# Eight start places for the split-weight buffers of a two-layer decoder kernel

## The chip, the cores and the metric

One core of a Trainium2 chip runs the whole program. The metric is device time in microseconds. Before the change the median of three runs is 1462.51 us (1461.71 to 1464.09).

## The reference

Two layers of a decoder trunk work on 512 tokens of width 1024, all in float32. What matters here is that nearly all the arithmetic is matrix products with weights:

```python
def hybrid_layer(x, g_mix, w_in, sinks, w_a, w_b, w_out, g_mlp, w_up, w_down):
    h = rmsnorm(x, g_mix)
    z = h @ w_in                       # 1024 x 5888, split into nine parts
    ...
    ya = sliding_window_sink_attention(aq, ak, av, sinks) @ w_a
    ...
    r = chunkwise_retention(rq, rk, rv)
    r = r * lax.rsqrt(jnp.mean(r * r, axis=-1, keepdims=True) + EPS)
    r = r.reshape(B, S, RET_V) * jax.nn.silu(rg.astype(jnp.float32))
    yb = r.astype(x.dtype) @ w_b
    mixed = jax.nn.sigmoid(ga) * ya + jax.nn.sigmoid(gb) * yb
    x = x + mixed @ w_out
    h2 = rmsnorm(x, g_mlp)
    x = x + jnp.square(jax.nn.relu(h2 @ w_up)) @ w_down
    return x
```

A last normalisation follows the second layer.

## The kernel before, in words

**Products.** Each float32 operand is split into a high part, rounded to the format `F32R`, and a low part, the rest. A product of two split operands is three matmuls, high by high, high by low and low by high (`products`, lines 390, 391 and 392; line 1296 for one of the matrices, line 405 in `by_halves`). Every matmul has two operands in SBUF: 128 x 128 **weights**, which TensorE loads first (the profile's PEld), and a **moving** operand of up to 512 columns, which it then streams through (the profile's PE). In the profile's names the moving operand stands first: `mm<-xh,hi` streams the activations `xh` past weights from `hi`, and `mm<-hi,r` streams weights of the model, `hi`, past activations in `r`. Weights of the next matmul are loaded while the present one streams.

**Units.** The model's weights come in units of 128 x 1024 numbers. The function `unit_order` writes their order out by hand. `split_until` (line 320) keeps three units ahead of the one in use: SyncE loads a unit into a `raw` buffer (five of them), ScalarE copies it, rounded, to a `hi` buffer (line 338), VectorE writes the rest to a `lo` buffer (line 339). There are `SPLIT + 1` = 4 buffers of `hi` and 4 of `lo`; units take them in turn. Some units are sums of others that VectorE or a DMA adds up first.

**Use of a unit.** Some functions take `hi` and `lo` as weights: `chunk`, `group` and `two_chunks` for `w_in`, `w_a`, `w_b` and `w_up` (512 moving columns), `pair` and `output` (256 columns). Others take them as the moving operand, with 512 columns: the `multiply` inside `down` (line 1534, tiles `mm<-hi,r` and `b<-hi,r`) and the one for the retention values (line 926, `rv<-hi,r`, `rv<-hi,xh`). Twelve to 24 matmuls or so read a unit before the next one comes.

**Places in SBUF.** The pools lay tiles out one behind the other in each partition. In the built program `raw`, `hi`, `lo`, `xh`, `xl`, the eight slots `r`, and all the temporary tiles of 2048 or 4096 bytes begin 128 bytes behind a multiple of 512: `hi` at byte 139,904, 144,000, 148,096 and 152,192, `lo` at 156,288, 160,384, 164,480 and 168,576. Tiles are multiples of 512 bytes long, and so are the steps inside them (a block of 128 weights is 512 bytes, a moving operand of 256 or 512 columns 1024 or 2048). The one large exception is `late` (line 157, 8192 bytes), a ninth slot that lies behind a few small tiles, at byte 220,224: 64 behind a multiple of 512. It is used as the slots `r` are, most often as a moving operand.

Of the kernel before, what the change touches and what calls it, by code (L numbers as in the profile page):

```python
# [11 lines left out]
F32R = mybir.dt.float32r  # L12
# [5 lines left out]
P = 128  # L18
# [26 lines left out]
N_BLOCK = 8  # L45
N_PAIR = 14
UNIT = 1024
WARM = 8
PACE = 0.8
DEEP = 3  # L50
# [2 lines left out]
SPLIT = 3  # L53
# [62 lines left out]
def decoder(ctx, tc, xT, x_first, w_in, w_rv, w_a, w_b, w_wo, w_up, w_pair, w_down, w_end, tables, decay, band, g_last, out):  # L116
# [4 lines left out]
    wpool = ctx.enter_context(tc.tile_pool(name="wpool", bufs=3))  # L121
# [6 lines left out]
    def f32(ap):  # L128
        return ap.bitcast(F32)
# [7 lines left out]
    def bank(pool, name):  # L137
        return pool.tile([P, T], F32, tag=pool.name, name=name)
# [27 lines left out]
    def halves(i):  # L166

        return (slice(0, UNIT // 2), slice(UNIT // 2, UNIT)) if i < 3 else (slice(0, UNIT),)

    def raw_tile():  # L170
        return wpool.tile([P, UNIT], F32, tag="raw", name="raw", bufs=5)

# [7 lines left out]
    def load_until(n):  # L180
        while state["loaded"] < min(n, len(order)):
            i = state["loaded"]
            layer, name, j = order[i][:3]
            if name == "pair":
                load_part(i)
            elif name == "block":
                load_block(i)
            elif name in MIXING:
                load_values(i)
            else:  # L190
                raws[i] = raw_tile()
                for at in halves(i):
                    queue = nc.scalar if i == 0 and at.start == 0 else nc.sync
                    source = w_end[j] if name == "w_end" else weights[name][layer, j]
                    queue.dma_start(raws[i][:, at], source[:, at])
                    if i < 3:
                        load_x()
            state["loaded"] += 1
# [3 lines left out]

    LEFT, RIGHT = slice(0, UNIT // 2), slice(UNIT // 2, UNIT)

    sums_up = [dram.tile([N_PAIR, P, UNIT], F32, name=f"sums_up{l}") for l in range(DEPTH)]
    sums_down = [dram.tile([N_BLOCK, P, 2 * UNIT], F32, name=f"sums_down{l}") for l in range(DEPTH)]
    sums_last = dram.tile([P, 2, UNIT], F32, name="sums_last")
    MIXING = {"rv": w_rv, "wo": w_wo}
# [67 lines left out]
    def add_part(i):  # L276
        if order[i][3] in (1, 2):
            last = raws.pop(i - 1)
            at = LEFT if order[i][3] == 1 else RIGHT
            nc.vector.tensor_tensor(raws[i][:, at], last[:, LEFT], last[:, RIGHT], ALU.add)  # L280
# [18 lines left out]
    def add_block(i):  # L299
        e, part = order[i][2:]  # L300
        if part in (2, 4) and e < N_BLOCK - 1:
            raws[i] = raws.pop(i - 2)
            nc.vector.tensor_tensor(raws[i], raws[i], raws.pop(i - 1), ALU.add)
# [10 lines left out]
    def add_values(i):  # L314
        part = order[i][2]
        if part in (2, 4):
            raws[i] = raws.pop(i - 2)
            nc.vector.tensor_tensor(raws[i], raws[i], raws.pop(i - 4), ALU.add)

    def split_until(n):  # L320
        while state["split"] < min(n, len(order)):
            i = state["split"]
            name, part = order[i][1], order[i][-1]
            if name in MIXING:
                add_values(i)
            load_until(i + AHEAD)
            if name == "pair":
                add_part(i)
            elif name == "block":
                add_block(i)  # L330
            raw = raws[i]
            hi = wpool.tile([P, UNIT], F32R, tag="hi", name="hi", bufs=SPLIT + 1)
            lo = wpool.tile([P, UNIT], F32R, tag="lo", name="lo", bufs=SPLIT + 1)
            for at in (LEFT,) if name == "pair" and part == 3 else halves(i):
                if i == 0 and at.start == 0:
                    nc.vector.tensor_copy(hi[:, at], raw[:, at])
                else:
                    state["high"] = nc.scalar.activation(hi[:, at], raw[:, at], AF.Copy).ins  # L338
                nc.vector.tensor_tensor(lo[:, at], raw[:, at], f32(hi[:, at]), ALU.subtract)  # L339
            kept = {  # L340
                "pair": part < 2,
                "block": name == "block" and part < 4 and order[i][2] < N_BLOCK - 1,
                **{n: name == n and order[i][2] < 4 for n in MIXING},
            }
            if not kept.get(name):
                raws.pop(i)
            parts[i] = (hi, lo)
            state["split"] += 1

    def unit(name, layer):  # L350
        i = state["next"]
        assert order[i][:2] == (layer, name), (order[i], layer, name)
        state["next"] += 1
        hold = state["hold"]
        split_until(i + SPLIT + 1 if hold is None else max(i + 1, min(hold, i + SPLIT + 1)))
        return parts.pop(i)
# [11 lines left out]
    warm = bank(ps_aux, "warm")  # L368
    for _ in range(WARM):
        nc.tensor.matmul(warm.rearrange("p (a b) -> p a b", b=P), ones, ones.unsqueeze(1).broadcast_to([P, 4, P]), start=True, stop=True)  # L370
# [243 lines left out]
    def layer_body(layer):  # L614
# [1006 lines left out]
        class Ending:  # L1621
# [74 lines left out]
            def first_weights(self):  # L1696
                with tc.issue_after(self.turned):
                    split_until(state["next"] + 1)
# [67 lines left out]

    scaled_input(0, 0)
    split_until(1)
    for u in (2, 3):
        for k in (2 * u - 3, 2 * u - 2):  # L1770
# [170 lines left out]
```

## Time and profile before

| | |
|---|---|
| runs | 1462.51, 1464.09, 1461.71 us |
| span of the profiled execution | 1462.3 us |
| TensorE matmuls (PE) | 8041, busy 1450.0 us, 99% of the span |
| TensorE weight loads (PEld) | 8041, busy 1265.4 us, 87% |
| VectorE (DVE) | 1762 instructions, busy 1169.0 us, 80% |
| ScalarE (ACT) | 1592 instructions, busy 969.0 us, 66% |
| GpSimd (POOL) | 329 instructions, busy 222.3 us, 15% |
| DMA | 297.57 MB, mean 203 GB/s |

The profiled execution's own time is its span, first to last instruction, 1462.3 us; it lies within the three runs, so what is worked out against it holds for the median as well. The duration of a matmul in the profile includes the time in which the next one is already streaming: two matmuls of 512 columns with durations of 389 ns begin about 227 ns apart. What adds up to the span is the distance from start to start, called **spacing** below; it is read from the start times in the timeline, over a stretch of several matmuls, since the timeline shows hundredths of a microsecond.

### The profile page before, as it was taken

The numbers are of one execution on the slowest core, as the hardware profiler recorded it, in microseconds if no ns is written. First come the engines' busy times: TensorE is split into PE (matmuls) and PEld (weight loads), VectorE is DVE, ScalarE is ACT, GpSimd is POOL, SyncE is SP. The second block draws the span as 40 slices with busy tenths as digits, with TensorE's granted clock in tenths as the row PEclk, the third lists the DMA queues.
The fourth block names the chain that finished last, engine by engine and source line by source line (L and its number), as shares of the span: only waits on it lengthen the run. The fifth ranks groups of instructions, "written<-read, shape, count | busy, mean of one in ns | idle before, by whom it ended". The sixth has DMA issues, their size and how long they took to land.

```text
span 1462.3 us, 22150 instructions
## 1 busy us (share of the span) xinstructions
PE 1450.0 (99%) x8041; PEld 1265.4 (87%) x8041; DVE 1169.0 (80%) x1762; ACT 969.0 (66%) x1592; POOL 222.3 (15%) x329
## 2 busy tenths in 40 slices
PE   9999999999999999999999999999999999999998
PEld 7888888888988999999888888888889799999997
DVE  6978876876898888888778788687778988788885
ACT  6657556543687777777756575565437777777775
POOL 0011012112101111111201110112120111111120
PEclk9999999999999999999999999999999999999999
DMA  7598369899745777666955983797885477777664
GB/s 257 177 288 225 103 174 299 232 244 255 224 119 195 192 197 190 165 184 179 307 178 172 290 222 111 217 291 219 222 210 174 137 198 201 191 192 197 178 185 146
DMA packets 96428, 297.57 MB, mean 203 GB/s; under 512 B 11328, under 2 KB 11456, under 8 KB 90432
## 3 DMA queue, kind: packets, MB, share of 16 engines
q0 software_dynamic: 35936, 125.58, 37.2%
q1 hardware_dynamic: 59664, 169.27, 33.4%
q8 instruction: 63, 1.03, 0.3%
q10 hardware_dynamic: 720, 1.31, 0.2%
q14 instruction: 45, 0.37, 0.1%
HBM read 256.54 MB, written 115.87 MB: 255 GB/s over the span
## 4 chain that ended last, share of the span: by engine, by line
PE 96%; ACT 1%; DMA 1%; DVE 1%; issue 0%; DVEq 0%; ACTq 0%
PE mm L390 23%; PE mm L391 23%; PE mm L392 23%; PE wo L1296 5%; PE b L390 3%; PE b L391 3%; PE b L392 3%; PE rv L392 2%; PE rv L390 2%; PE rv L391 2%; PE mm L405 2%; PE score L773 1%; PE pT L738 1%; PE r L392 1%; PE r L391 1%; PE r L390 1%
## 5 line engine op out<-in xcount | busy, mean ns | idle before, releaser
L338 ACT ACTIVATE hi<-raw 128x1024 fp32r<-128x1024 f32 (+1 forms) x387 | 394.1, 1021 | 263.4 <-PE mm L391 146.9
L339 DVE TENSOR_TENSOR lo<-raw,hi 128x1024 fp32r<-128x1024 f32 (+1 forms) x388 | 452.7, 1174 | 107.4 <-ACT hi L338 105.3
L390 PE MATMUL mm<-xh,hi 128*128 128x512 f32 (+1 forms) x976 | 343.8, 356 | 1.8 <-ACT xh L413 1.0
L391 PE MATMUL mm<-xl,hi 128*128 128x512 f32 (+1 forms) x976 | 344.6, 356 | 0.0
L392 PE MATMUL mm<-xh,lo 128*128 128x512 f32 (+1 forms) x976 | 340.4, 355 | 0.0
L390 PEld LDWEIGHTS mm<-xh,hi 128*128 128x128 f32 x976 | 185.2, 190 | 27.7 <-ACT xh L413 1.7
L391 PEld LDWEIGHTS mm<-xl,hi 128*128 128x128 f32 x976 | 185.3, 190 | 24.2
L392 PEld LDWEIGHTS mm<-xh,lo 128*128 128x128 f32 x976 | 183.9, 190 | 23.6
L391 PE MATMUL mm<-r,hi 128*128 128x256 f32 (+1 forms) x608 | 189.2, 311 | 0.0
L392 PE MATMUL mm<-r,lo 128*128 128x256 f32 (+1 forms) x608 | 189.0, 311 | 0.0
L390 PE MATMUL mm<-r,hi 128*128 128x256 f32 (+1 forms) x608 | 186.6, 311 | 0.5 <-ACT mm L1471 0.5
L390 PEld LDWEIGHTS mm<-r,hi 128*128 128x128 f32 x608 | 115.8, 190 | 8.8 <-ACT mm L1471 0.7
L391 PEld LDWEIGHTS mm<-r,hi 128*128 128x128 f32 x608 | 115.8, 190 | 8.0
L392 PEld LDWEIGHTS mm<-r,lo 128*128 128x128 f32 x608 | 115.8, 190 | 6.3
L1619 POOL DMA_DIRECT2D y<-eu x56 | 62.4, 1354 | 374.4 <-DVE eu L1604 373.8
L391 PE MATMUL mm<-lo,r 128*128 128x512 f32 (+1 forms) x276 | 104.3, 387 | 0.0
L392 PE MATMUL mm<-hi,r 128*128 128x512 f32 (+1 forms) x276 | 101.3, 387 | 0.0
L390 PE MATMUL mm<-hi,r 128*128 128x512 f32 (+1 forms) x276 | 98.4, 390 | 0.9 <-ACT eu L1614 0.6
L390 PE MATMUL b<-hi,r 128*128 128x512 f32 x180 | 70.5, 392 | 1.6 <-DVE eu L1604 1.2
L391 PE MATMUL b<-lo,r 128*128 128x512 f32 x180 | 70.3, 390 | 0.0
L1296 PE MATMUL wo<-r,hi 128*128 128x256 f32 x384 | 69.4, 283 | 0.0
L392 PE MATMUL b<-hi,r 128*128 128x512 f32 x180 | 67.9, 390 | 0.0
(323 smaller groups left out, 2682.5 us busy)
## 6 DMA issues: line engine op xcount, KB each, us to landing
raw<-w_in_in SPq DMA_DIRECT2D x73, 512.0 KB, 5.8
sums_down<-w_down_in POOLq DMA_DIRECT2D x30, 1024.0 KB, 11.6
sums_up<-w_pair_in POOLq DMA_DIRECT2D x56, 512.0 KB, 10.9
raw<-w_down_in SPq DMA_DIRECT2D x45, 512.0 KB, 7.6
raw<-w_pair_in SPq DMA_DIRECT2D x84, 256.0 KB, 3.7
y<-y POOLq DMA_DIRECT2D x63, 256.0 KB, 9.4
y<-eu POOLq DMA_DIRECT2D x61, 256.0 KB, 8.1
raw<-sums_down SPq DMA_DIRECT2D x30, 512.0 KB, 7.4
```

Of the source, the lines that this page charges most:

```text
L338: state["high"] = nc.scalar.activation(hi[:, at], raw[:, at], AF.Copy).ins
L339: nc.vector.tensor_tensor(lo[:, at], raw[:, at], f32(hi[:, at]), ALU.subtract)
L390: nc.tensor.matmul(ps, ah, bh, start=start and i == 0, stop=False, **more)
L391: nc.tensor.matmul(ps, ah, bl, start=False, stop=False, **more)
L392: latest[0] = nc.tensor.matmul(ps, al, bh, start=False, stop=stop and i == n - 1, **more).ins
L405: latest[0] = nc.tensor.matmul(ps, w[:, cols(j, c)], moving[k][low], start=first, stop=bool(final)).ins
L738: nc.tensor.transpose(pt[:, i * P : (i + 1) * P], sm[:, at : at + P], ident)
L773: nc.tensor.matmul(ps[:, g * w : (g + 1) * w], q_s[g][:, c, at], part[:, keys], start=i == 0, stop=i == 1)
L1296: latest[0] = nc.tensor.matmul(o, w[:, cols], v, start=start and first and n % 2 == 0 and w is hi and v is vh, stop=final and w is lo, ski ...
L1619: nc.gpsimd.dma_start(y[:, 2 * j + m, i * T : (i + 1) * T], t, **how)
```

## The change

Each `hi` and each `lo` buffer becomes 16 numbers (64 bytes) longer, and the kernel uses the first 1024 numbers of it as before:

```diff
@@ -45,6 +45,7 @@
 N_PAIR = 14
 UNIT = 1024
+LINE = 16
 WARM = 8
@@ -329,8 +330,9 @@
             raw = raws[i]
-            hi = wpool.tile([P, UNIT], F32R, tag="hi", name="hi", bufs=SPLIT + 1)
-            lo = wpool.tile([P, UNIT], F32R, tag="lo", name="lo", bufs=SPLIT + 1)
+            hi, lo = (
+                wpool.tile([P, UNIT + LINE], F32R, tag=n, name=n, bufs=SPLIT + 1)[:, :UNIT] for n in ("hi", "lo")
+            )
             for at in (LEFT,) if name == "pair" and part == 3 else halves(i):
```

In the built program the buffers lie 4160 bytes apart instead of 4096. Their places behind a multiple of 512 bytes become

| buffer | 1 | 2 | 3 | 4 |
|---|---|---|---|---|
| `hi` | 128 | 192 | 256 | 320 |
| `lo` | 384 | 448 | 0 | 64 |

Everything behind them moves by 8 x 64 = 512 bytes and so keeps its place behind a multiple of 512: `late` stays at 64, all the other operands at 128. The instructions of every engine, their order and their waits are the same before and after.

## The prediction

> **What bounds the kernel now.** I read the view of the cores first, with the granted clock of TensorE, then the page: its busy times and the chain that ended last.
>
> ```profile
> core 0: 1462.3 us, clock 0.999
> ...
> span 1462.3 us, 22150 instructions
> PE 1450.0 (99%) x8041; PEld 1265.4 (87%) x8041; DVE 1169.0 (80%) x1762; ACT 969.0 (66%) x1592; POOL 222.3 (15%) x329
> ...
> PE 96%; ACT 1%; DMA 1%; DVE 1%; issue 0%; DVEq 0%; ACTq 0%
> ```
>
> TensorE is busy for 99% of the span, at a granted clock of 0.999, and holds 96% of the chain. So the time is the sum of the spacings of 8041 matmuls, and waits for other engines are a few per cent. The list of waits says the same from the other side: ScalarE, which fills `hi`, most often waits for a matmul to free a buffer.
>
> ```profile
> ACT hi L338 <- PE mm L391: 146.9, 95, 4.5
> ```
>
> The splitting is ahead of TensorE, so a change pays or costs only through the spacing of matmuls. Which ones have an operand in a split buffer is in the groups of instructions, kept apart by shape; the columns that I use are the shape and the count, then busy time and mean duration.
>
> ```profile
> L390 PE MATMUL mm<-xh,hi 128*128 128x512 f32 x640 | 249.2, 394 | 1.6 <-ACT xh L413 1.0 <-DVE rot L635 0.6
> L390 PE MATMUL mm<-r,hi 128*128 128x512 f32 x160 | 59.9, 390 | 0.0
> L390 PE MATMUL mm<-late,hi 128*128 128x512 f32 x32 | 12.7, 396 | 0.0
> L405 PE MATMUL mm<-xh,hi 128*128 128x512 f32 x32 | 8.2, 393 | 0.0
> L390 PE MATMUL mm<-hi,r 128*128 128x512 f32 x268 | 96.2, 393 | 0.9 <-ACT eu L1614 0.6 <-ACT r L410 0.2
> L390 PE MATMUL b<-hi,r 128*128 128x512 f32 x180 | 70.5, 392 | 1.6 <-DVE eu L1604 1.2 <-ACT r L410 0.4
> L390 PE MATMUL rv<-hi,r 128*128 128x512 f32 x64 | 24.9, 389 | 0.0
> L390 PE MATMUL rv<-hi,xh 128*128 128x512 f32 x48 | 18.7, 389 | 0.0
> ...
> L390 PE MATMUL mm<-r,hi 128*128 128x256 f32 x448 | 126.7, 283 | 0.5 <-ACT mm L1471 0.5
> L390 PE MATMUL mm<-xh,hi 128*128 128x256 f32 x336 | 94.6, 283 | 0.1
> L1296 PE MATMUL wo<-r,hi 128*128 128x256 f32 x384 | 69.4, 283 | 0.0
> L1296 PE MATMUL wo<-r,lo 128*128 128x256 f32 x192 | 54.2, 283 | 0.0
> ```
>
> Each row of line 390 or 405 stands for three, one for each of the three part products. With 512 columns, split buffers are the weights in 3 x (640 + 160 + 32 + 32) = 2592 matmuls and the moving operand in 3 x (268 + 180 + 64 + 48) = 1680: **4272** together. With 256 columns they are weights in 3 x (448 + 336) + 384 + 192 = 2928, and in 96 more past `late`: **3024**. So 7296 of the 8041 matmuls are touched, and one nanosecond on each is 7.3 us.
>
> **What a start place costs.** The kernel before holds an experiment of its own. `late` begins at 64 behind a multiple of 512 bytes, every other operand at 128. The timeline of TensorE passes from one to the other twice in short order, first with 512 columns. (Start in us, duration, instruction; the rows left out follow in the same rhythm.)
>
> ```profile
> 317.41 0.39 PE L390 MATMUL mm<-late,hi 128*128 128x512 f32 x1
> ...
> 319.51 0.39 PE L392 MATMUL mm<-xh,lo 128*128 128x512 f32 x1
> ...
> 321.12 0.39 PE L390 MATMUL mm<-xh,hi 128*128 128x512 f32 x1
> ...
> 322.48 1.07 PE L390 MATMUL mm<-r,hi 128*128 128x512 f32 x4
> ```
>
> Nine matmuls past `late` take 2.10 us, 233.3 ns each. The next seven stream `xh` again, at the same place as the weights, and still take 1.61 us, 230.0 ns each: the rhythm settles only slowly. The six behind them take 1.36 us, 226.7 ns each, and that is what undisturbed stretches keep. Now 256 columns:
>
> ```profile
> 402.94 0.28 PE L1296 MATMUL wo<-r,hi 128*128 128x256 f32 x1
> ...
> 403.90 0.40 PE L1296 MATMUL wo<-late,hi 128*128 128x256 f32 x2
> ...
> 405.28 0.39 PE L1296 MATMUL wo<-r,hi 128*128 128x256 f32 x2
> ...
> 405.98 0.40 PE L1296 MATMUL wo<-r,hi 128*128 128x256 f32 x2
> ```
>
> Eight matmuls at equal places take 0.96 us (120.0 ns each), the twelve past `late` 1.38 us (115.0), the six behind them 0.70 us (116.7). So a difference of 64 bytes between moving operand and weights makes a matmul of 512 columns **6.6 ns slower** and one of 256 columns **5.0 ns faster**, and a change of places costs the one 3.3 ns and gains the other 3.3 ns for some matmuls more. I read this as the two reads of TensorE meeting in SBUF, with a phase that settles; the trace shows the sizes, not the cause.
>
> **The change part by part.** It adds and removes no instruction, DMA or wait, so all of its effect is in durations. Writers and readers on the other engines come first. VectorE and ScalarE write `late` at 64 from operands at 128 as they write `r`; medians stand between the smallest and the largest duration.
>
> ```profile
> L411 DVE TENSOR_TENSOR r<-rot,r x10: 680/684/692, 155.0 to 1001.2; 128x512 fp32r<-128x512 f32 x10
> L411 DVE TENSOR_TENSOR late<-rot,late x6: 668/684/692, 122.0 to 984.1; 128x512 fp32r<-128x512 f32 x6
> ...
> L410 ACT ACTIVATE r<-rot x10: 612/624/634, 153.2 to 998.0; 128x512 fp32r<-128x512 f32 x10
> L410 ACT ACTIVATE late<-rot x6: 612/622/634, 120.8 to 981.9; 128x512 fp32r<-128x512 f32 x6
> ```
>
> 684 ns both times on VectorE, 624 and 622 on ScalarE: I cost the splits at nothing. If a split did get slower, ScalarE's waits for TensorE above are the cover, and beyond them it would be TensorE that waits for `hi`. DMAs write only `raw`, which doesn't move.
>
> That leaves the 7296 matmuls. One buffer of the eight stays at 128, so seven eighths get an unequal pair of places; and since a unit's `lo` lies 256 bytes off its `hi` and part products take `hi`, `hi`, `lo` in turn, places now change all the time. The trace shows 64 bytes one way and the change back; it doesn't show 128, 192 or 256. For these I take the mean of the two unequal states that it shows. **512 columns:** between 230.0 and 233.3 is 231.7, 5.0 ns over 226.7; 4272 x 7/8 x 5.0 = 18.7 us. Part of that is there already, since stretches are disturbed now wherever shapes change: the group means of 390 to 394 ns above stand 1 to 5 over the undisturbed 389, waits included, and I take 1 ns of it off as rhythm, 3.7 us. **256 columns:** between 115.0 and 116.7 is 115.9, 4.1 under 120.0; 3024 x 7/8 x 4.1 = 10.8 us gained. The sum is 18.7 - 3.7 - 10.8 = **+4.2 us**, 1466.7 us from the median, and I say 1467.
>
> The ends, which I keep for the range. Dearest: all unequal 512-column matmuls at 233.3 and no gain at 256, 4272 x 7/8 x 6.6 = 24.7 us, 1487. Cheapest: the extra 256 columns cost 226.7 - 120.0 = 106.7 ns, so streaming 512 alone would be 213.4, and 13.3 ns of each spacing are overhead; if half of it went, as nearly happens at 256 columns, that is 4272 x 7/8 x 6.6 = 24.7 us, with 3024 x 7/8 x 5.0 = 13.2 us from 256 columns, 1425. Nothing in the trace shows a stretch of 512-column matmuls under 226.7.
>
> **A rule that speaks against any effect.** The Trainium skill, in "TensorE: Matmul & The Clock Gate" under "Step-by-step: what each phase is for", says that weights and moving operand come through two independent read ports of SBUF, so that loading the next weights takes no read bandwidth from the running matmul. By that rule the start places are indifferent and the sum would be 0, 1462.5 us. The rows of `late` disagree: 233.3 against 226.7 ns with nothing else changed, at a clock of 0.999. It stays a rival, with a chance of 0.05, in so far as the effect may belong to `late` itself.
>
> **Rivals.**
> - *Mixed places free the weight loads and cost 512 columns nothing* (the other side: faster). For it: the 256-column matmuls gain in both unequal states, and a settled equal pair may be the one that meets at every load. Against it: both unequal states cost at 512 columns. Price: the 13.2 us above, 1449, or down to 1425 with a gain at 512 columns. It decides when 512-column matmuls lose, net of today's disturbance, less than 10.8 us / (4272 x 7/8) = 2.9 ns.
> - *Loss and gain cancel, or places matter little beyond `late`*: 1460 to 1465. For it: the two terms above are of one size and opposite sign. Against it: that would be chance.
> - *Only the moving operand's place counts.* Then half of the 1680 moving reads stand, like `late`, at an odd multiple of 64: 840 x 6.6 = 5.5 us, 1468, and 256 columns gain nothing. It ends beside my forecast, and is counted with it.
>
> That the change doesn't do what it says is excluded by the places in the built program, and `late` keeps its own.
>
> **How the numbers follow.** A measurement of this kernel tells about 0.2% (2.9 us) from no change. My forecast, 512 columns losing more than 256 columns gain, has a chance of 0.50, from just over 1465 to 1490. The faster rival has 0.34, from 1425 to just under 1460. Cancelling (0.11) or no effect (0.05) has 0.16. The range that leaves out a tenth at each end is 1441 to 1488: it holds the forecast up to its dearest end and the faster rival past its 1449.
>
> **What would show it.** In the trace after, stretches of `mm<-xh,hi` with 512 columns at 229 to 233 ns and not in a settled 226.7, varying from unit to unit with period four; `wo<-r,hi` at 113 to 118 and not 120; unchanged rows of lines 338, 339 and `late`. If 512-column stretches stay at 226.7, or fall, the sum is wrong by its largest term and the kernel is faster; if 256 columns stay at 120, it is slower by up to 11 us more. Wholly wrong would be a change in the waits, or in the VectorE rows.

## The result, and the profile after

The changed kernel takes **1470.31 us** (median of three runs, 1470.08 to 1470.33), against 1462.51 before: a ratio of 1.0049, 95% interval 1.003 to 1.0069. It is slower, by 7.8 us where the prediction said 4.5 (1467 us; its sum gave 4.2). From here on **difference** means the place where the weights begin minus the place where the moving operand begins, modulo 256 bytes.

The view of the cores and the page of the kernel after show the same picture as before, only longer.

```profile
core 0: 1468.3 us, clock 0.999
...
span 1468.3 us, 22150 instructions
PE 1455.9 (99%) x8041; PEld 1258.9 (86%) x8041; DVE 1168.5 (80%) x1762; ACT 969.7 (66%) x1592; POOL 222.4 (15%) x329
...
PE 96%; ACT 2%; DMA 1%; DVE 1%; issue 0%; SPq 0%; DVEq 0%; ACTq 0%
```

The clock is the same, VectorE and ScalarE are busy within 1 us of what they were, and TensorE still holds 96% of the chain. What has grown is TensorE's own line. The list of waits and the rows of the splits say the same:

```profile
ACT hi L340 <- PE mm L393: 143.2, 94, 4.5
...
L340 ACT ACTIVATE hi<-raw 128x1024 fp32r<-128x1024 f32 x354 | 373.5, 1058 | 255.8 <-PE mm L393 140.2 <-issue 41.5 <-PE rv L394 23.5
L341 DVE TENSOR_TENSOR lo<-raw,hi 128x1024 fp32r<-128x1024 f32 x354 | 430.0, 1219 | 92.2 <-ACT hi L340 91.2 <-PE wo L1298 0.2
```

ScalarE still waits mostly for TensorE to free a buffer, and a split into the moved buffers costs 1058 and 1219 ns (before: 1058 and 1221). So the loss is in the spacing. In the timeline of the kernel after, five units of 24 matmuls follow each other, with 512 columns, as weights; the rows are the first of each unit and the first matmul behind the last one (start, duration, instruction).

```profile
155.04 0.39 PE L392 MATMUL mm<-xh,hi 128*128 128x512 f32 x1
...
160.64 0.39 PE L392 MATMUL mm<-r,hi 128*128 128x512 f32 x1
...
166.09 0.39 PE L392 MATMUL mm<-r,hi 128*128 128x512 f32 x1
...
171.59 0.40 PE L392 MATMUL mm<-r,hi 128*128 128x512 f32 x1
...
177.18 0.39 PE L392 MATMUL mm<-r,hi 128*128 128x512 f32 x1
...
182.78 0.39 PE L924 MATMUL rv<-xh,ones 128*128 128x512 f32 x1
```

Divided by 24, the steps of 5.60, 5.45, 5.50, 5.59 and 5.60 us are spacings of 233.3, 227.1, 229.2, 232.9 and 233.3 ns. The buffers stand at the differences 64, 0, 192, 128 and 64: a period of four units, in which only the equal place keeps the old spacing. Now 256 columns, in four units of 24 and, from 463.04 on, in two halves of 12:

```profile
368.68 0.40 PE L1298 MATMUL wo<-r,hi 128*128 128x256 f32 x2
...
371.50 0.40 PE L1298 MATMUL wo<-r,hi 128*128 128x256 f32 x2
...
374.33 0.40 PE L1298 MATMUL wo<-r,hi 128*128 128x256 f32 x2
...
377.19 0.40 PE L1298 MATMUL wo<-r,hi 128*128 128x256 f32 x2
...
380.05 0.40 PE L1298 MATMUL wo<-r,hi 128*128 128x256 f32 x2
...
463.04 0.28 PE L392 MATMUL mm<-r,hi 128*128 128x256 f32 x1
...
464.40 0.28 PE L392 MATMUL mm<-r,hi 128*128 128x256 f32 x1
...
465.84 0.28 PE L392 MATMUL mm<-r,hi 128*128 128x256 f32 x1
```

The units stand at differences of 64, 192, 128 and 0, and their spacings are 117.5, 117.9, 119.2 and 119.2 ns. The half unit from 463.04, at 192, has 1.36 us / 12 = 113.3 ns, and the one behind it, at 0, 120.0. So the same difference gave 117.9 in one place and 113.3 in another: there are **two rhythms** (a rhythm is a sequence of distances that repeats). The short one, in the minority here (of 2714 stretches of six distances 439 have a mean under 114.2 ns), is the one that the prediction had seen in part beside `late`: of its twelve distances there the first four are 121, 122, 115 and 115 ns and the last eight 113.4 on average.

I took the distances from start to start over the whole trace, leaving out the few with a wait in them (over 245 ns with 512 columns, over 135 ns with 256):

| matmuls | before, mean ns | after, mean ns | effect |
|---|---|---|---|
| 512 columns, split buffer as weights, 2435 | 227.98 | 230.96 | +7.3 us |
| 512 columns, split buffer as moving operand, 1609 | 227.63 | 231.41 | +6.1 us |
| 256 columns, 2983 | 119.59 | 117.64 | -5.8 us |

The sum is +7.6 us, beside 7.8 between the medians. The two profiled spans differ by only 6.0, since the one of before holds something that is not in that table. The rows are those of the first twelve matmuls behind the warm-up and the one that follows them, of before and then of after.

```profile
5.84 2.08 PE L390 MATMUL mm<-xh,hi 128*128 128x512 f32 x4 [1.00 <-ACT xh L413]
7.72 1.91 PE L391 MATMUL mm<-xl,hi 128*128 128x512 f32 x4
9.43 1.16 PE L392 MATMUL mm<-xh,lo 128*128 128x512 f32 x4
10.43 0.40 PE L390 MATMUL mm<-xh,hi 128*128 128x512 f32 x1
```

```profile
5.71 1.17 PE L392 MATMUL mm<-xh,hi 128*128 128x512 f32 x4 [1.08 <-ACT xh L415]
...
8.54 0.39 PE L392 MATMUL mm<-xh,hi 128*128 128x512 f32 x1
```

The same twelve matmuls take 4.59 us in the one and 2.83 in the other. A start that is 1.8 us longer fits the runs of before, which fall into two groups, near 1462.1 and near 1464.2. The profiled execution of before belongs to the upper one: in that of after the measured time lies 2.0 us above the span (1470.31 and 1468.3), and 1462.3 + 2.0 is 1464.3. So its span does not stand for the median, though it lies among the three times; the table is not touched by this, since it compares distances. The trace's record of the granted clock goes with it: its first entry, the full clock, begins at 9.57 us in the trace of before and at 4.26 in that of after. In all fourteen traces of this case it begins between 9.57 and 10.11 us where the twelve matmuls take 4.6 to 4.9 us (before and three others), at 6.53 where they take 3.4, and between 4.00 and 5.41 where they take 2.8 to 2.9.

### The profile page after: what moved, and what is told of

Its sections match the earlier page's. It is cut to its first block, busy times and chain, and to the rows that moved or that the text cites. A ratio compares the mean times of both kernels' runs of the same rounds, so it can differ in the third digit from the quotient of the medians.

```text
span 1468.3 us, 22150 instructions
## 1 busy us (share of the span) xinstructions
PE 1455.9 (99%) x8041; PEld 1258.9 (86%) x8041; DVE 1168.5 (80%) x1762; ACT 969.7 (66%) x1592; POOL 222.4 (15%) x329
## 4 chain that ended last, share of the span: by engine, by line
PE 96%; ACT 2%; DMA 1%; DVE 1%; issue 0%; SPq 0%; DVEq 0%; ACTq 0%
PE mm L392 23%; PE mm L393 23%; PE mm L394 23%; PE wo L1298 5%; PE b L392 3%; PE b L393 3%; PE b L394 3%; PE rv L394 2%; PE rv L392 2%; PE rv L393 2%; PE mm L407 2%; PE score L775 1%; PE pT L740 1%; PE r L393 1%; PE r L394 1%; PE r L392 1%
```

## The experiments

The theory after the result: *the difference alone sets the spacing; 0 is best with 512 columns and worst with 256*. Its rivals: places that change from unit to unit are what costs; the place of one operand alone counts; 512 bytes is the period; and the order of instructions on other engines, which some edits shift, makes the differences.

**All eight buffers moved by one distance.** Two unused tiles, one ahead of the buffers and one behind, shift them and nothing else that is large:

```diff
+            if i == 0:
+                wpool.tile([P, 16], F32, tag="front", name="front", bufs=1)
             hi = wpool.tile([P, UNIT], F32R, tag="hi", name="hi", bufs=SPLIT + 1)
             lo = wpool.tile([P, UNIT], F32R, tag="lo", name="lo", bufs=SPLIT + 1)
+            if i == 0:
+                wpool.tile([P, 112], F32, tag="behind", name="behind", bufs=1)
```

> All eight split buffers begin 64 bytes further on, at 192 behind a multiple of 512; all other operands stay at 128. Theory A (what counts is the difference between the weights' place and the moving operand's place): it is constant here and unequal, so undisturbed stretches of 512 columns with split weights run at 233.3 ns and not at 226.7, those with a split moving operand at about 229, 256 columns at 113 to 118 and not at 120. By count 2496 x 5.5 + 1680 x 1.4 us/1000 = 16.1 us lost and 2928 x (1.8 to 6.2) = 5 to 18 us gained: 1460 to 1473 us. Theory B (a place is indifferent, changing it from one unit to the next costs): 226.7 and 120 ns, 1462.5 us.

With 64 bytes: 1469.22 us, ratio 1.0036 (1.0023 to 1.0049). Nothing changes from unit to unit here, and it still costs 5.5 us between the medians. Every unit of 512-column weights is at 233.3 ns in its timeline (24 matmuls in 5.60 us):

```profile
161.91 0.39 PE L394 MATMUL mm<-r,hi 128*128 128x512 f32 x1
...
167.51 0.39 PE L394 MATMUL mm<-r,hi 128*128 128x512 f32 x1
...
173.11 0.39 PE L394 MATMUL mm<-r,hi 128*128 128x512 f32 x1
```

Over the trace: 233.2 ns as weights, 229.7 as moving operand (where the difference is 192), 115.8 with 256 columns.

> All eight split buffers begin at 384 behind a multiple of 512, 256 bytes off every other operand. Theory A with a period of 256 bytes: this pair is equal again, 226.7 and 120.0 ns, 1462.5 us, as before. Theory A with a period of 512 bytes: 256 is as unequal as can be; with the 232 and 118.6 ns that an unequal pair keeps, 4272 x 4.4 - 2928 x 1.0 = 16 us, 1478 us.

With 64 numbers in each of the two tiles, so 256 bytes: 1463.76 us, ratio 0.9997 (0.9988 to 1.0007), and the same stretch is back at 226.7 ns (5.44 us for 24).

```profile
160.63 0.39 PE L394 MATMUL mm<-r,hi 128*128 128x512 f32 x1
...
166.07 0.39 PE L394 MATMUL mm<-r,hi 128*128 128x512 f32 x1
...
171.51 0.39 PE L394 MATMUL mm<-r,hi 128*128 128x512 f32 x1
```

The two kernels have the same order of instructions, and differ in places alone. So the loss comes from the place, without any change of it, and the period is 256 bytes and not 512.

**Places chosen per unit.** Buffers with 64 numbers to spare allow a start for each unit. The room comes from one of seven temporary tiles, so a base without any offset comes first:

```diff
-        return tmp.tile([P, T], F32, tag="t", name=name, bufs=7)
+        return tmp.tile([P, T], F32, tag="t", name=name, bufs=6)
...
-            hi = wpool.tile([P, UNIT], F32R, tag="hi", name="hi", bufs=SPLIT + 1)
-            lo = wpool.tile([P, UNIT], F32R, tag="lo", name="lo", bufs=SPLIT + 1)
+            at0 = 0
+            hi, lo = (
+                wpool.tile([P, UNIT + 64], F32R, tag=n, name=n, bufs=SPLIT + 1)[:, at0 : at0 + UNIT] for n in ("hi", "lo")
+            )
```

> Base for later runs: each split buffer is 256 bytes longer and is used from its start, so that places alternate between 128 and 384; the room comes from the temporary tiles, six buffers and not seven. If the period is 256 bytes and six temporaries suffice, 226.7 and 120.0 ns and 1462.5 us. If the period is 512, every second unit is unequal: half of 16 us, 1470 us. If the temporaries were needed, TensorE waits for ScalarE or VectorE, which the waits would show.

1467.32 us, ratio 1.0027 (1.0017 to 1.0037). The spacings are those of before (226.7 and 120 settled), and its TensorE has waits that before doesn't have, 2.4 of the 3.6 us lost in these two rows alone:

```profile
PE mm L392 <- ACT hi L340: 1.4, 3, 0.7
...
PE mm L392 <- DVE z L990: 1.0, 1, 1.0
```

The base is thus no kernel before: the order of instructions differs too, on TensorE at 604 of 8041 places. What stands on it is compared with it.

> As the base with slack, but the units that are used with 256 moving columns begin 64 bytes further on; those used with 512 columns stay at an equal place. Theory A: 512 columns keep 226.7 ns, 256 columns run at 113.4 to 117.8, so 2928 x (1.8 to 6.2) = 5 to 18 us are gained: 1444 to 1457 us. Theory B (changing places costs, no place is better): no gain in settled stretches, and losses where 256 and 512 columns meet: 1462 to 1468 us.

Edit: `at0 = 16 if name in ("wo", "pair") else 0`, so that only units used with 256 columns begin 64 bytes on. 1462.34 us, ratio to before 0.9993 (0.9983 to 1.0004): 5.0 us under its base. 512 columns stay at 226.7 ns, 256 columns fall from 119.6 to a mean of 117.1. The time alone would speak for Theory B, since it was expected from a base of 1462.5 us; the spacings decide. By them the gain is 2983 x 2.5 ns = 7.5 us. That only 5.0 are seen is not explained in full; TensorE's waits for `hi` grow from 1.4 to 2.1 us.

> As the run with 256-column units 64 bytes on, but only their high part moves; the low part stays at an equal place. Part products take high, high, low in turn. If each weight load is paid by its own difference, two thirds of the gain of that run: 1467.3 - 3.3 = 1464.0 us, with 117.8 and 120 ns in one stretch. If a change of place inside the stretch disturbs it, less or nothing: 1467 us; if it moves the phase into the shorter of the two rhythms seen (113.3), more: 1458 us.

Edit: as above, for `hi` only. 1464.02 us, ratio 1.0006 (0.9996 to 1.0015). All three part products take 117.8 ns, the `lo` one too, whose own difference is 0: the spacing is a rhythm of the sequence, not a price of each matmul. That the time is the 1464.0 us forecast for such a price is chance, since the 120 ns that belong to it are not there.

> On the base with slack: the change's loss alone. Units used with 512 columns begin 0, 64, 128 or 192 bytes into their buffer by turns; units used with 256 columns always at 0. If loss and gain add up (the trace of the change gives +3.0 ns on 2435 matmuls with split weights and +3.8 on 1609 with a split moving operand, against -1.9 on 2983 with 256 columns), this is the base and 13.3 us: 1467.3 + 13.3 = 1480.6 us, with 120 ns at 256 columns. If units disturb each other where they meet, the base and 8 us only, as in the whole change: 1475 us.

Edit: `at0 = 0 if name in ("wo", "pair") else 16 * (i % 4)`, the opposite. 1481.2 us, ratio 1.0124 (1.0109 to 1.0139), 13.9 us over its base (timed on another chip) where 13.3 were expected: 231.0 ns as weights, 231.6 as moving operand, 119.6 with 256 columns. The loss of the one kind and the gain of the other exist separately.

> On the base with slack: each unit begins 16 bytes further into its buffer than the one before, 0 to 240 and round again, so that every difference in steps of 16 bytes is seen in the settled end of some unit. If the period of 256 bytes is made of lines of 64 bytes, spacings come in four levels (512 columns with split weights 226.7, 233.3, 232, 229 ns at 0, 64, 128, 192) with steps between them; if lines are 16 bytes or the phase is continuous, they move by a few tenths to 2 ns with each 16 bytes, and some place may undercut 226.7 at 512 or 113.3 at 256 columns. Its total means little: 1470 to 1482 us.

Edit: `at0 = 4 * (i % 16)`, steps of 16 bytes over one period, a single run: 1480.03 us. Mean of the last five distances of each stretch, in ns, for twelve of the sixteen differences:

| difference | 0 | 16 | 32 | 64 | 96 | 128 | 160 | 176 | 192 | 208 | 224 | 240 |
|---|---|---|---|---|---|---|---|---|---|---|---|---|
| 512, weights | 227.1 | 231.5 | 233.1 | 233.5 | 234.1 | 233.3 | 233.7 | 230.1 | 229.7 | 232.4 | 233.5 | 228.0 |
| 256 | 119.8 | 118.6 | 118.1 | 113.3 | 118.1 | 118.8 | 120.0 | 118.1 | 117.2 | 116.7 | 116.8 | 118.5 |

No place gives 512 columns less than the equal one, and 16 bytes on already cost 4 ns. With few stretches to a value and two rhythms, single values of the lower row mean little; the shape does not follow steps of 64 bytes.

> Another base: split buffers 256 bytes longer, used from their start, seven temporaries as before; the room comes from the two tiles sh and sl, which become halves of one of the six large temporaries. If the 3.6 us of the first base come from the missing temporary, 1463 us; if they come from the order that the scheduler finds when anything changes in the pools, 1466 us or so again.

An attempt at a better base: seven temporary tiles kept, and `sh` and `sl` made halves of one large temporary tile instead.

```diff
-        sh = tmp.tile([P, T], F32R, tag="sh", name="sh", bufs=1)
-        sl = tmp.tile([P, T], F32R, tag="sl", name="sl", bufs=1)
+        both = big("sh", F32R)
+        sh, sl = both[:, 0, :], both[:, 1, :]
```

1479.96 us, ratio 1.0117 (1.01 to 1.0133), far from both expected times. TensorE now waits for that tile, among others:

```profile
PE ssq L570 <- ACT sh L412: 8.9, 4, 3.8
```

Around two of these waits the granted clock is 0.50, from 309.2 to 316.0 us and from 1043.1 to 1049.8; 18 matmuls of 512 columns in these stretches are about 427 ns apart, which makes 3.6 us more. Everywhere else the spacings are unchanged. The run tells nothing of places, only that pools here are not to be touched lightly.

**The order kept.** The last four leave the order of every engine's instructions exactly as before. Only `hi` gets 48 numbers more, and a table says which buffer a unit gets, so that its start can be brought back to an equal place:

```diff
+BUFFER = "0321032103210321..."
...
-            hi = wpool.tile([P, UNIT], F32R, tag="hi", name="hi", bufs=SPLIT + 1)
+            at0 = (16 * int(BUFFER[i]) + (16 if name in ("wo", "pair") else 0)) % 64
+            hi = wpool.tile([P, UNIT + 48], F32R, tag="hi", name="hi", bufs=SPLIT + 1)[:, at0 : at0 + UNIT]
```

> A control: the hi buffers are 4288 bytes apart, but every unit begins 128 behind a multiple of 256, so all places are equal again, and the order of every engine is that of before. Theory (the difference of the two operands' start places modulo 256 bytes sets the spacing): the time of before, 1462 to 1464 us, 512 columns settled at 226.7 ns, 256 columns at 120.0. Rival (longer buffers or their distance cost something themselves): above 1466 us.

With 0 in place of the 16: 1462.42 us, ratio 0.9997 (0.9988 to 1.0006). Longer buffers by themselves cost nothing.

> As the control, but units that are used with 256 columns begin 64 bytes on, in the hi buffers alone. Theory: 512 columns stay at 226.7 ns, the 2983 matmuls of 256 columns fall from a mean of 119.6 ns to between 117.8 (one of the two rhythms seen, as with hi alone moved before) and 115.8 (both, as with all eight buffers moved), so the time falls by 5.4 to 11.3 us against the control, to 1451 to 1458 us. Rival (the gain was one of the other order of instructions): within 1.5 us of the control.

As shown: **1457.26 us**, ratio 0.9961 (0.9949 to 0.9974), 5.2 us under the control and faster than both kernels. Its timeline keeps 226.7 ns with 512 columns (24 in 5.44 us) and has 117.7 with 256 (96 in 11.30 us):

```profile
159.28 0.39 PE L392 MATMUL mm<-r,hi 128*128 128x512 f32 x1
...
164.72 0.39 PE L392 MATMUL mm<-r,hi 128*128 128x512 f32 x1
...
364.20 0.40 PE L1298 MATMUL wo<-r,hi 128*128 128x256 f32 x2
...
375.50 0.40 PE L1298 MATMUL wo<-r,hi 128*128 128x256 f32 x2
```

Of the two ends expected, the time took the dear one: with `hi` alone moved, the short rhythm of 113.3 does not hold here. The rival of another order falls.

> As the one before, but 192 bytes on in place of 64. Theory: 256 columns at 117.2 to 117.8 ns, 5.4 to 7.2 us less than the control, 1455 to 1458 us. If the sign of the difference decides between the two rhythms, this one and the one 64 on differ by up to 6 us; otherwise they are equal.

With 48 in place of the 16: 1457.82 us, ratio 0.9965 (0.9952 to 0.9977), 117.8 ns. The sign of the difference does not matter for `hi` alone.

> The opposite of the narrow ones: units that are used with 512 columns begin 64 bytes on, those used with 256 stay equal. Theory, with the spacings of the run with all eight buffers 64 on: as weights 233.2 in place of 228.0 ns on 2435 matmuls, as moving operand 229.7 in place of 227.6 on 1609, 12.7 + 3.4 = 16 us more than the control, 1478 to 1480 us. Rival (only the moving operand's place counts): 3.4 us more, 1466 us.

With the 16 and the 0 exchanged: 1482.44 us, ratio 1.0134 (1.0121 to 1.0148), 20.0 us over the control, above what was expected and far above the 1466 us of the rival that only the moving operand's place counts. As weights the spacing is 232.7 ns, a little under the 233.2 taken; as moving operand it is 232.6 and not 229.7. The two timelines show the same work, 18 matmuls with the retention values as moving operand, first with all buffers 64 on:

```profile
197.53 0.39 PE L394 MATMUL rv<-hi,r 128*128 128x512 f32 x1
...
201.65 0.39 PE L394 MATMUL rv<-hi,r 128*128 128x512 f32 x1
```

and then with only `hi` 64 on:

```profile
192.15 0.39 PE L392 MATMUL rv<-hi,r 128*128 128x512 f32 x1
...
196.34 0.40 PE L392 MATMUL rv<-hi,r 128*128 128x512 f32 x1
```

4.12 us are 228.9 ns each, 4.19 us are 232.8. In the second kernel `hi` stands at 192 and `lo` at 0, and the sequence of both is dearer than either alone (229 and 226.7). 2.9 ns on 1609 matmuls are 4.7 us, less 0.5 ns on 2435, 1.2 us: this is the surplus, 3.5 us, where the medians have 4.0. So the theory has to be narrowed: the difference sets the spacing where it is constant; where it changes from matmul to matmul, the sequence does.

## Why the prediction was right

**What bounds the kernel, and that only spacing could change:** as said. Busy times of the other engines, the waits and the clock stood still.

**The sign of both effects, from `late`:** right, and it was the difference, not `late` itself. The prediction kept the Trainium skill's rule as a rival ("TensorE: Matmul & The Clock Gate", "Step-by-step: what each phase is for": two independent read ports of SBUF), by which places would be indifferent. The two kernels with all buffers moved disagree with it: places differ, orders do not, and 226.7 ns become 233.3. In the kernel after, buffers that happen to share the place of `late` bring it back to the old spacing. Twelve matmuls past `late` at the difference 0 take 1.43 us, 119.2 ns each, where before took 115.0; all but the first are 120 ns apart:

```profile
1134.03 0.40 PE L1298 MATMUL wo<-late,hi 128*128 128x256 f32 x2
...
1135.46 0.40 PE L1298 MATMUL wo<-r,hi 128*128 128x256 f32 x2
```

Only such stretches tell the difference from the weights' own place, since every other operand stands at 128; they are few.

**The share of unequal pairs, seven eighths:** wrong, it is three quarters. The prediction counted places modulo 512, took `hi` and `lo` of one unit for unequal, and so expected places to change all the time. Modulo 256 the two are equal, as the kernel moved by 256 bytes shows, and within a unit nothing changes.

**The 512-column term, 18.7 - 3.7 = 15.0 us:** measured 13.4. The mean of 231.7 ns for unknown unequal places was close: with a quarter of the matmuls left at the old mean, the other three have 232.0 as weights and 232.7 as moving operand. But this was luck. Of the two states behind that mean only 233.3 belongs to an unequal place; 230.0 was read where places were equal again and the rhythm was still settling. That the middle of the two lies near the 233.3, 232.9 and 229.2 ns that 64, 128 and 192 gave is chance. The 1 ns taken off as rhythm fits: the means of before lie 1.3 and 0.9 ns over 226.7.

**The 256-column term, -10.8 us: the step that failed in size.** Measured -5.8. Three quarters instead of seven eighths makes it -9.3 (and the 512-column term 16.0 - 3.7 = 12.3, the sum +3.0, so that the wrong share brought the forecast nearer to what was measured). The rest is the spacing itself: unequal pairs have (117.64 - 119.59 / 4) / 0.75 = 117.0 ns, 2.6 under the mean of before, where 115.9 and 4.1 under 120.0 were forecast. The stretch beside `late` had gone over into the rhythm of 113.3 ns, which most units of the kernel after do not reach, and the 116.7 behind it was again a settling at equal places and no unequal state. Of the difference between the forecast 4.2 us and the 7.6 of the table, this term makes +5.0 and the other -1.6.

**The rivals.** *Mixed places free the loads*: it was to decide at a net loss below 2.9 ns per unequal 512-column matmul; by the same count it is 13.4 us / (4272 x 7/8) = 3.6, and the gain it counted on was half as large. *Loss and gain cancel*: they are 13.4 and 5.8. *Only the moving operand's place counts*: with all buffers 64 on, matmuls whose moving operand never moved went from 228.0 to 233.2 ns, so it falls, though its 1468 us lay nearer to the measured 1470.31 than the forecast did.

Why the difference counts at all stays open. The runs show its sizes, its period and the rhythms; that two reads meet in SBUF was only argued.

## What to carry to other kernels

When TensorE is the bound, look at where both operands of its matmuls begin, relative to each other: here equal places were best with 512 columns and worst with 256, and choosing the place by use gained 0.4% where eight places in turn, whatever the use, lost 0.5%. An operand that happens to lie elsewhere, as `late` did, is an experiment that the trace already holds, but its price is to be read from long stretches. And before a size is changed to get a place, run the size without the place: the room taken from a pool cost 3.6 us between the medians here, and the place gained 5.0.

## What the runs showed of the hardware

- The spacing of matmuls depends on the difference of the two operands' start places with a period of 256 bytes: 226.7 ns at 0, 233.3 at 64 (512 columns, split buffers as weights); 120.0 at 0, 113.3 or 117.8 at 64 (256 columns).
- It is a rhythm of the whole sequence. Moving the operand of two part products in three moves all three, and equal places in a mixed sequence lose their advantage: 232.6 ns where constant places have 226.7 and 229.
- At a granted clock of 0.50 matmuls of 512 columns begin 427 ns apart (18 of them, in the run with `sh` and `sl` in one tile), where they take 227 at 1.00. Each of the two stretches goes with a wait of TensorE of almost 4 us; the longest single wait of TensorE in the trace of before is 1.2 us, and no entry of 0.50 stands there before the last matmul has ended.
- The first matmuls behind the warm-up can take as long, 428 ns (four in the 1.71 us from 7.72 to 9.43 in the trace of before). The view of stretches gives a clock of 1.00 there, but the trace has no entry of the clock before 9.57 us, where these matmuls end. In the trace of after the entries begin at 4.26 us, ahead of them, and but for the first they take about 230. What decides when the full clock comes was not tried.
